# Output projection: a chunk's transposes, weight scaling and operand stores written behind the next chunk's matmuls

## The chip, the core and the metric

The kernel runs on one core of a Trainium2 chip. The metric is the device time of one execution in microseconds (us). The engines named below are PE (matmuls and transposes; PEld is its weight load), DVE (elementwise work and reductions), ACT (scalar engine: casts, squares, scaling by a column), POOL (small vectors here) and SP, whose queue issues the DMAs. Each engine works through its own list of instructions in order.

## The reference, cut to what matters

One encoder block on 2048 tokens of width 1024. Two mixers give `y1` (1024 columns) and `y2` (512 columns). What follows them is the part that this change touches:

```python
h = h + jnp.concatenate([y_ssd, y_s5], axis=-1) @ w_out[i]
h = h + conv_ffn(rms_norm(h, norm_ffn_w[i]), ffn_w_up[i], ffn_conv_w[i],
                 ffn_conv_b[i], ffn_w_down[i])
return rms_norm(h, norm_final_w)
```

`rms_norm` divides a row by the root of its mean square and multiplies it by a weight per column; `conv_ffn` is an up projection, a convolution of width 3, a gate and a down projection.

## The kernel before

The program has three long parts: the mixers (up to about 1200 us), the output projection (16 chunks of 128 tokens, 1206 to 1620 us) and the FFN (the rest). The change lies in the second part and at its border to the third. Below, G0 to G15 are the matmuls of the 16 chunks.

**One chunk of the output projection.** `out_pre` prepares the left operand. It loads `z`, `y`, `c` and the decay of the chunk, multiplies `c` by the running state `fst` on PE (tile `po`, 8 products, two records each), adds that to `y` (lines 852, 853), carries the state on (lines 862, 863), multiplies by `z` (854), and splits the result into a high and a low part (`yh` on ACT, `yl` on DVE, lines 443, 444; the 512 columns of `y2` in lines 876, 877). It also sums the squares (tiles `sqr`, `pn`, `ssq`) and makes two row factors on POOL (`rsq`). `out_gemm` then runs 72 matmuls of 128x512: 12 blocks of the depth, two halves `n` of the columns, three products each (`yh*wh`, `yh*wl`, `yl*wh`; `mm3`, lines 448 to 450). They end in the four tiles `p1`, `p2` of the two halves. DVE adds them to `x` in `xto` (912, 913), SP stores the sum (914). Then comes the norm in front of the FFN: ACT squares the row and sums it (917), POOL makes the factor (`rstd`, lines 435 to 440), ACT scales the row into `h2` (919).

**The tail of a chunk** is the loop over `q` at the end of `out_gemm`: per half, four PE transposes of `h2` into the one buffer `pth` (927), four scalings by the norm's weight into `hT` (ACT for the first half, line 933; DVE for the second, 931) and one store into `hop_d` (934), the right operand of the FFN. Since `pth` has one buffer, the second four transposes wait until ACT has emptied it. Below, Tc is the pair of transpose blocks of chunk c.

**The FFN** is a list of jobs (`strassen`). The first 22 jobs use tokens 0 to 1023, that is the `hop_d` rows of chunks 0 to 7 and the sums of them that `tok_sums` makes in chunks 9 to 12. The first job needs two blocks of `w_up` (tile `wr`, line 1090) with their sums and splits on DVE and ACT (`left_ops`), and 14 loads `tst` of the right operand (1020), each split into `th` (ACT, 1022) and `tl` (DVE, 1023). The loads of all these parts share one pool of 13 buffers (`tag="g4"`).

**Order.** The program text sets a priority; a scheduler then orders every engine's list ahead of time. In the text, chunk `ch + 1` is prepared before chunk `ch` is multiplied:

```python
for ch in range(15):
    cur = pre
    pre = b.out_pre(sp, gp, ps, pp, ch + 1)
    b.out_gemm(sp, gp, ps, pp, ch, *cur)
```

Of the kernel before, what the change touches and what calls it, by code (L numbers as in the profile page):

```python
# [9 lines left out]
F32 = mybir.dt.float32  # L10
# [4 lines left out]
PSUM = bass.MemoryType.PSUM  # L15
DRAM = bass.MemoryType.DRAM

P = 128
L = 2048
D = 1024  # L20
# [395 lines left out]
NG4 = 13  # L416
# [4 lines left out]
class Block:  # L421
# [476 lines left out]
    def out_gemm(self, sp, sq, ps, pp, ch, yh, yl, rs):  # L898
        nc = self.nc
        v = nc.vector  # L900
        t0 = 128 * ch
        xt = sq.tile([P, D], F32, name="xto", tag="g4", bufs=NG4)
        nc.sync.dma_start(xt, self.A["x"][0, t0:t0 + P, :])
        for n in range(2):
            c = slice(512 * n, 512 * n + 512)
            p1 = ps.tile([P, 512], F32, name="p1", tag="mm")
            for k in range(8):
                self.mm3(p1, (yh[:, k], yl[:, k]), [w[:, k, c] for w in self.wo], k == 0, k == 7)
            p2 = ps.tile([P, 512], F32, name="p2", tag="mm")
            for k in range(4):  # L910
                self.mm3(p2, (yh[:, 8 + k], yl[:, 8 + k]), [w[:, 8 + k, c] for w in self.wo], k == 0, k == 3)
            v.scalar_tensor_tensor(xt[:, c], p1, rs[:, 0:1], xt[:, c], ALU.mult, ALU.add)
            v.scalar_tensor_tensor(xt[:, c], p2, rs[:, 1:2], xt[:, c], ALU.mult, ALU.add)
        nc.sync.dma_start(self.x2_d[t0:t0 + P, :], xt)
        h2 = sp.tile([P, D], F32, name="h2", bufs=2)
        s2 = sp.tile([P, 2], F32, name="ssn", bufs=2)
        nc.scalar.activation(h2, xt, AF.Square, accum_out=s2[:, 0:1])
        self.rstd(s2[:, 1:2], s2[:, 0:1], self.rtmp(sp, "rtmq"), 1.0 / D)
        nc.scalar.activation(h2, xt, AF.Copy, scale=s2[:, 1:2])
        hop = self.hop_d[ch // 8]  # L920
        t1 = 128 * (ch % 4)
        for q in range(2):
            pt = pp.tile([P, 4, P], F32, name="pth", bufs=1)
            cur = sq.tile([P, 4, P], F32, name="hT", tag="g2", bufs=NG2)
            for j in range(4):
                k = 4 * q + j
                nc.tensor.transpose(pt[:, j], h2[:, 128 * k:128 * k + 128], self.ident)
            for j in range(4):
                w = self.nfw[:, 4 * q + j:4 * q + j + 1]
                if q:  # L930
                    v.tensor_scalar(cur[:, j], pt[:, j], w, None, ALU.mult)
                else:
                    nc.scalar.activation(cur[:, j], pt[:, j], AF.Copy, scale=w)
            nc.sync.dma_start(hop[:, (5 if q else 7) if ch % 8 > 3 else q, :, t1:t1 + P], cur)
# [92 lines left out]
    def strassen(self, pu, pd, sp, jobs):  # L1027

        nc = self.nc
        copy = lambda src: self.copied(sp, src)  # L1030
        def prod(ps, j, o, first):
            kt, mm = j["kt"], nc.tensor.matmul
            for k in range(kt):
                l, r = j["L"][o](k), j["R"][o](k)
                for i, (x, y) in enumerate(((l[0], r[0]), (l[0], r[1]), (l[1], r[0]))):
                    mm(ps, x, y, start=first and k == i == 0, stop=k == kt - 1 and i == 2, skip_group_check=not first)  # L1036
        def first(j):
            j["A"] = pu.tile([P, 512], F32, name="pA", bufs=2)
            prod(j["A"], j, 0, True)
            p1 = copy(j["A"])  # L1040
            pD = pu.tile([P, 512], F32, name="pD", bufs=2)
            prod(pD, j, 1, True)
            j["take"](0, 0, pD, p1)
        def middle(j):
            prod(j["A"], j, 2, False)
            j["u2"] = copy(j["A"])
            j["B"] = pd.tile([P, 512], F32, name="pB", bufs=2)
            prod(j["B"], j, 3, True)
            prod(j["A"], j, 4, False)
            j["take"](1, 1, j["B"], copy(j["A"]))  # L1050
        def end(j):
            prod(j["A"], j, 5, False)
            j["take"](0, 1, j["A"], None)
            prod(j["B"], j, 6, False)
            j["take"](1, 0, j["B"], j["u2"])
            j["done"]()
        prev = R = None
        jobs[0]["L"] = jobs[0]["left"]()
        for i, j in enumerate(jobs):
            if j["right"]:  # L1060
                if prev:
                    end(prev)
                prev = None
                R = j["right"]()
            j["R"] = R
            if i + 1 < len(jobs):
                jobs[i + 1]["L"] = jobs[i + 1]["left"]()
            first(j)
            if prev:
                end(prev)  # L1070
            middle(j)
            prev = j
            if j.get("after"):
                j["after"]()
        end(prev)
# [108 lines left out]
def hybrid_block_kernel(ctx: ExitStack, tc: tile.TileContext, *aps):  # L1184
    nc = tc.nc
    A = dict(zip(_INS, aps[:-1]))
    b = Block(nc, tc, A, aps[-1])
    pool = tc.tile_pool
    right = lambda name: tc.tile_pool(name=name, bufs=1, side="right")
# [4 lines left out]
    with ExitStack() as mix:  # L1194
        en = mix.enter_context
        mc = en(pool(name="mixc", bufs=1))
# [3 lines left out]
        pp = psa.enter_context(pool(name="pp", bufs=1, space=PSUM, side="right"))  # L1200
        ps, p5 = (psg.enter_context(pool(name=n, bufs=2, space=PSUM)) for n in ("psmm", "ps5"))
# [39 lines left out]
        with pool(name="s5v", bufs=1) as vp, ExitStack() as xs:  # L1241
# [7 lines left out]
            sp = rs.enter_context(right("sp"))  # L1249
# [39 lines left out]
        ps = psb.enter_context(pool(name="psb", bufs=4, space=PSUM))  # L1289
        rs.close()  # L1290
        psa.close()
        pp = psc.enter_context(pool(name="ppb", bufs=1, space=PSUM, side="right"))
        gp = en(tc.tile_pool(name="gp", bufs=1, side="right", reuse_waits="tile"))
        with right("b1") as sp:
            pre = b.out_pre(sp, gp, ps, pp, 0)
            for ch in range(15):
                cur = pre
                pre = b.out_pre(sp, gp, ps, pp, ch + 1)
                b.out_gemm(sp, gp, ps, pp, ch, *cur)
                if 9 <= ch < 13:  # L1300
                    b.tok_sums(gp, 0, ch - 9)
            b.ffn_consts(mc, gp, ps)
            b.out_gemm(sp, gp, ps, pp, 15, *pre)
        wo.close()
        psb.close()
        pu = en(pool(name="psu", bufs=4, space=PSUM))
# [4 lines left out]
        b.ffn_late(fs)  # L1311
        jobs = [b.up_job(ft, gp, fs, s, f) for s in range(2) for f in range(b.NF)]
        jobs += [b.down_job(ft, gp, fs, c, i) for c in range(3) for i in range(8)]
        b.strassen(pu, pd, fs, jobs)


# [34 lines left out]
```

## Time and profile before

| | |
|---|---|
| median of 3 runs | 2987.97 us (2986.86 to 2992.83) |
| the profiled execution | 2995.89 us, span in the trace 2994.1 us |
| PE busy over the span | 2743.8 us (92%), 12952 matmul records |
| DVE, ACT, POOL busy | 2213.7, 1365.9, 659.3 us (74%, 46%, 22%) |
| mean granted clock of PE | 0.959 of full speed |
| output projection, first matmul of G0 to last of G15 | 1205.87 to 1609.76 us |
| first matmul of the FFN | 1619.65 us |

The span is what the trace covers of the profiled execution; the rest of its time lies around it. Matmuls are pipelined, so the distance from one start to the next tells more than the duration of one record. A granted clock of 1 stands for 2.4 GHz, 0.5 for 1.2 GHz; values between are means over a stretch.

### The profile page before, as it was taken

To read this page: it belongs to the slowest core of one execution; us is meant where nothing else is said; L and a number is where in the kernel's file an instruction comes from. 1 tells how busy PE (TensorE), PEld (TensorE's weight loads), DVE (VectorE), ACT (ScalarE), POOL (GpSimd) and SP (SyncE) were. 2 spreads that over 40 slices of the span, in tenths; PEclk is the share of its full clock that TensorE was granted. 3 is DMA by queue.
4 is the path that set the end of the run, shared out by engine and by line. 5 is a ranking of instruction groups with operands and counts; after the bars stand their busy time and mean duration, and the time that the engine had idled before them with its cause. 6 is when DMAs were issued, how large, how long until landed. Compare 5 with 4: busy or idle time off the path is not lost. (4 is left out here: it accounts for less than half of the span.)

```text
span 2994.1 us, 37277 instructions
## 1 busy us (share of the span) xinstructions
PE 2743.8 (92%) x12952; PEld 2196.2 (73%) x12952; DVE 2213.7 (74%) x3287; ACT 1365.9 (46%) x2329; POOL 659.3 (22%) x1133
## 2 busy tenths in 40 slices
PE   6999899787999997787988999999999999999997
PEld 4556899665878886676766887787877877877775
DVE  5997488786787776655766777778878878656586
ACT  4532355455567665333334444446444445233254
POOL 0543299993133322112111000000000000000012
PEclk9999999887999999898889999999999999999999
DMA  4545734448456656956865223425433446565464
GB/s 126 166 120 157 199 101 125 111 138 221 130 164 175 189 162 209 224 162 176 223 192 163 78 94 118 134 85 189 148 113 126 134 134 216 178 204 189 150 222 152
DMA packets 507145, 471.55 MB, mean 157 GB/s; under 512 B 90108, under 2 KB 417100, under 8 KB 506956
## 3 DMA queue, kind: packets, MB, share of 16 engines
q1 hardware_dynamic: 504716, 463.99, 51.8%
q0 software_dynamic: 2240, 5.18, 0.7%
q8 instruction: 102, 1.67, 0.2%
q14 instruction: 87, 0.71, 0.1%
HBM read 324.37 MB, written 144.67 MB: 157 GB/s over the span
## 5 line engine op out<-in xcount | busy, mean ns | idle before, releaser
L1036 PE MATMUL pA<-th,lh 128*128 128x512 f32 x1056 | 424.5, 403 | 36.2 <-ACT pc L1079 34.0
L1036 PE MATMUL pA<-tl,lh 128*128 128x512 f32 x1056 | 421.6, 399 | 2.4 <-DVE tl L1023 2.3
L1036 PE MATMUL pA<-th,ll 128*128 128x512 f32 x1056 | 420.8, 399 | 1.5 <-DVE ll L444 1.4
L448 PE MATMUL pmm<-hh,wh 128*128 128x512 f32 (+1 forms) x896 | 335.2, 374 | 6.3 <-DVE zt L709 3.1
L449 PE MATMUL pmm<-hl,wh 128*128 128x512 f32 (+1 forms) x896 | 334.8, 374 | 0.0
L450 PE MATMUL pmm<-hh,wl 128*128 128x512 f32 (+1 forms) x896 | 331.7, 370 | 0.0
L1036 PEld LDWEIGHTS pA<-th,lh 128*128 128x128 f32 x1056 | 201.4, 191 | 96.3 <-ACT pc L1079 46.1
L1036 PEld LDWEIGHTS pA<-tl,lh 128*128 128x128 f32 x1056 | 201.8, 191 | 51.1 <-DVE tl L1023 4.7
L1036 PEld LDWEIGHTS pA<-th,ll 128*128 128x128 f32 x1056 | 201.2, 191 | 50.5 <-DVE ll L444 2.7
L1036 PE MATMUL pB<-tl,lh 128*128 128x512 f32 x528 | 208.8, 395 | 2.6 <-DVE tl L1023 2.6
L1036 PE MATMUL pB<-th,lh 128*128 128x512 f32 x528 | 208.6, 395 | 1.6 <-ACT lh L443 1.6
L1036 PE MATMUL pB<-th,ll 128*128 128x512 f32 x528 | 208.3, 395 | 0.0
L448 PEld LDWEIGHTS pmm<-hh,wh 128*128 128x128 f32 x896 | 170.6, 190 | 37.3 <-issue 5.7
L1079 ACT COPY pc<-pA 128x512 f32<-128x512 f32 x204 | 114.8, 581 | 181.2 <-PE pA L1036 180.6
L449 PEld LDWEIGHTS pmm<-hl,wh 128*128 128x128 f32 x896 | 170.5, 190 | 26.2 <-issue 5.9
L450 PEld LDWEIGHTS pmm<-hh,wl 128*128 128x128 f32 x896 | 170.4, 190 | 24.5 <-issue 4.4
L767 ACT ACTIVATE Lt<-rw,tokS 128x128 f32<-128x128 f32 x512 | 157.6, 389 | 56.9 <-PE pyd L773 44.9
L695 DVE SCALAR_TENSOR_TENSOR xbc<-rb,cw,xbc 128x1024 f32<-128x1024 f32 x128 | 176.0, 1378 | 3.5 <-ACT xbc L693 2.4
L448 PE MATMUL p<-wo,yh 128*128 128x512 f32 x384 | 162.3, 423 | 13.8 <-ACT yh L443 13.8
L443 ACT CAST lh<-s 128x512 fp32r<-128x512 f32 (+3 forms) x136 | 109.9, 815 | 126.7 <-DVE s L1003 63.2
L444 DVE TENSOR_TENSOR ll<-s,lh 128x1024 fp32r<-128x1024 f32 (+3 forms) x136 | 126.2, 931 | 49.5 <-PE pA L1036 41.3
L449 PE MATMUL p<-wo,yh 128*128 128x512 f32 x384 | 160.4, 418 | 0.0
(421 smaller groups left out, 6206.2 us busy)
## 6 DMA issues: line engine op xcount, KB each, us to landing
wr<-in_ffn_w_up_dram SPq DMA_DIRECT2D x88, 512.0 KB
rw<-acs_d SPq DMA_DIRECT2D x128, 256.0 KB
wraw<-in_w_in_dram SPq DMA_DIRECT2D x52, 512.0 KB
ar<-act_d SPq DMA_DIRECT2D x32, 512.0 KB
yp_d<-cv SPq DMA_DIRECT2D x32, 512.0 KB
cv<-yp_d SPq DMA_DIRECT2D x32, 512.0 KB
tst<-hop_d SPq DMA_DIRECT2D x28, 512.0 KB
act_d<-cv SPq DMA_DIRECT2D x22, 512.5 KB
```

The costliest lines, as they stand in the source:

```text
L443: self.nc.scalar.copy(hi, src)
L444: self.nc.vector.tensor_tensor(lo, src, hi.bitcast(F32), ALU.subtract)
L448: mm(ps, lhs[0], rhs[0], start=first, stop=False)
L449: mm(ps, lhs[0], rhs[1], start=False, stop=False)
L450: mm(ps, lhs[1], rhs[0], start=False, stop=last)
L695: nc.vector.scalar_tensor_tensor(ac, rb[:, j:j + 1024], cw(j), ac, ALU.mult, ALU.add)
L767: nc.scalar.activation(Lt[:, d, h], rw[:, d, h], AF.Exp, bias=tk(0, d, h))
L1036: mm(ps, x, y, start=first and k == i == 0, stop=k == kt - 1 and i == 2, skip_group_check=not first)
L1079: self.nc.scalar.copy(t, src)
```

## The change

The loop over `q` becomes a function of its own, `out_tail`. In the text the tail of chunk `ch - 1` now stands behind the matmuls of chunk `ch`; the tail of chunk 15 is called in the middle of the first FFN job, and its `h2` takes a buffer of the shared pool, since its own pool is closed by then. `pth` gets a PSUM pool of its own that stays open. `ffn_consts` moves ahead of the last chunk's matmuls and `tok_sums` one chunk later.

```diff
         nc.sync.dma_start(self.x2_d[t0:t0 + P, :], xt)
-        h2 = sp.tile([P, D], F32, name="h2", bufs=2)
+        if ch < 15:
+            h2 = sp.tile([P, D], F32, name="h2", bufs=2)
+        else:
+            h2 = sq.tile([P, D], F32, name="h2", tag="g4", bufs=NG4)
...
+        return h2
+
+    def out_tail(self, sq, pt_, ch, h2):
...
         for q in range(2):
-            pt = pp.tile([P, 4, P], F32, name="pth", bufs=1)
+            pt = pt_.tile([P, 4, P], F32, name="pth", bufs=1)
...
             first(j)
+            if j.get("mid"):
+                j["mid"]()
             if prev:
...
+        pth = en(pool(name="pth", bufs=1, space=PSUM, side="right"))
...
-            for ch in range(15):
+            h2 = None
+            for ch in range(16):
                 cur = pre
-                pre = b.out_pre(sp, gp, ps, pp, ch + 1)
-                b.out_gemm(sp, gp, ps, pp, ch, *cur)
-                if 9 <= ch < 13:
-                    b.tok_sums(gp, 0, ch - 9)
-            b.ffn_consts(mc, gp, ps)
-            b.out_gemm(sp, gp, ps, pp, 15, *pre)
+                if ch < 15:
+                    pre = b.out_pre(sp, gp, ps, pp, ch + 1)
+                else:
+                    b.ffn_consts(mc, gp, ps)
+                last, h2 = h2, b.out_gemm(sp, gp, ps, pp, ch, *cur)
+                if ch:
+                    b.out_tail(gp, pth, ch - 1, last)
+                if 10 <= ch < 14:
+                    b.tok_sums(gp, 0, ch - 10)
...
+        jobs[0]["mid"] = lambda: b.out_tail(gp, pth, 15, h2)
```

The scheduler decides what this does to each list. First PE, before, from the last matmuls of chunk 3 to the first of chunk 4 (`p_11778` is a result tile of chunk 3, `p_11892` and `p_11917` of chunk 4, `h_11794` is `h2` of chunk 3):

```order
L448 MATMUL p_11778<-wo_10988,yh 128x512
L449 MATMUL p_11778<-wo_10989,yh 128x512
L450 MATMUL p_11778<-wo_10988,yl 128x512
L849 MATMUL po<-ctt,fst 128x128 x8
L927 MATMUL pth<-ident,h_11794 128x128 x8
L448 MATMUL p_11892<-wo_10988,yh 128x512
L449 MATMUL p_11892<-wo_10989,yh 128x512
L448 MATMUL p_11917<-wo_10988,yh 128x512
```

All eight transposes of chunk 3 stand between the two chunks, right behind the state products `po`. The odd chunks 1 to 13 read like this; the tails of the even chunks 0 to 14 stand as two blocks of four among the next chunk's matmuls already.

Now PE after the change: first around the state products inside chunk 4 (`p_11913`, one of its result tiles), then from chunk 4 (`p_11938`) to chunk 5 (`p_12052`, `p_12077`), with `h_11775` the `h2` of chunk 3.

```order
L448 MATMUL p_11913<-wo_10988,yh 128x512
L449 MATMUL p_11913<-wo_10989,yh 128x512
L849 MATMUL po<-ctt,fst 128x128 x8
L450 MATMUL p_11913<-wo_10988,yl 128x512
L448 MATMUL p_11913<-wo_10988,yh 128x512
L449 MATMUL p_11913<-wo_10989,yh 128x512
```

The products stand 25 matmuls ahead of the chunk's end, and the left operand of chunk 5 hangs on them. From the end of chunk 4 on:

```order
L449 MATMUL p_11938<-wo_10989,yh 128x512
L450 MATMUL p_11938<-wo_10988,yl 128x512
L936 MATMUL pth<-ident,h_11775 128x128 x4
L448 MATMUL p_12052<-wo_10988,yh 128x512
L449 MATMUL p_12052<-wo_10989,yh 128x512
L448 MATMUL p_12077<-wo_10988,yh 128x512
```

A first block of transposes still stands between two chunks, but it is that of the chunk before; the second block follows 20 matmuls later. The tails of chunks 1, 5, 9 and 11 keep a row of eight, one chunk later than before. Behind the state products of a chunk stand, up to the next chunk's first matmul, 25 matmuls in chunks 4, 5, 8 and 9, 21 and a row of eight in chunk 12, 13 and a row of eight in chunk 6, 6 and a row of eight in chunk 2; in chunk 10 it is 5 matmuls, a row of eight and the state products of one more chunk. In chunks 0, 1, 3, 7, 11 and 13 they stand earlier; chunk 14's have 23 behind them, and no chunk follows the next. Behind G15 stand five transposes of chunk 14 and four of chunk 15, then the FFN's first 110 matmuls, then the last four transposes.

Then SP's queue from the end of the output projection into the FFN, before:

```order
L914 DMA x_d<-xto 128x1024
L1090 DMA wr<-in_ffn_w_up_dram 128x8x128 x2
L934 DMA hop_d<-hT 128x4x128
L840 DMA ctt<-ct_d 128x4x128
L934 DMA hop_d<-hT 128x4x128
L1020 DMA tst<-hop_d 128x1024 x2
L914 DMA x_d<-xto 128x1024
L1020 DMA tst<-hop_d 128x1024
L934 DMA hop_d<-hT 128x4x128
L1020 DMA tst<-hop_d 128x1024
L934 DMA hop_d<-hT 128x4x128
L985 DMA nlw<-in_norm_final_w_dram 128x1024
```

and after the change:

```order
L943 DMA hop_d<-hT 128x4x128 x2
L994 DMA nlw<-in_norm_final_w_dram 128x1024
L914 DMA x_d<-xto 128x1024
L943 DMA hop_d<-hT 128x4x128
L1101 DMA wr<-in_ffn_w_up_dram 128x8x128 x2
L943 DMA hop_d<-hT 128x4x128
L1029 DMA tst<-hop_d 128x1024 x14
L1101 DMA wr<-in_ffn_w_up_dram 128x8x128 x4
L943 DMA hop_d<-hT 128x4x128 x2
```

`nlw` is the load that can only start when G15 has ended. Before, the first two loads `wr` and four loads `tst` stand ahead of it; now all of them stand behind it, and behind the store of chunk 15's `xto`.

Last DVE at the same border, before (`p_13943` is the last result tile of chunk 15):

```order
L913 SCALAR_TENSOR_TENSOR xto<-p_13943,rsq,xto 128x512
L931 TENSOR_SCALAR hT<-pth,nfw 128x128 x4
L1003 TENSOR_TENSOR s_14016<-wr,s_14015 128x512
L1023 TENSOR_TENSOR tl_14038<-tst,th_14037 128x1024 x2
L1023 TENSOR_TENSOR tl_14048<-tst,th_14047 128x1024 x2
```

and after the change (`p_13924` is the last result tile of chunk 15):

```order
L913 SCALAR_TENSOR_TENSOR xto<-p_13924,rsq,xto 128x512
L940 TENSOR_SCALAR hT<-pth,nfw 128x128 x4
L1009 TENSOR_TENSOR s_13996<-wr 128x512
L1010 TENSOR_TENSOR s_13996<-s_13996,wr 128x512
L1011 TENSOR_TENSOR wr<-wr 128x512
L444 TENSOR_TENSOR ll<-wr,lh 128x1024
L1012 TENSOR_TENSOR s_13997<-wr,s_13996 128x512
L444 TENSOR_TENSOR ll<-s_13996,lh 128x1024
L444 TENSOR_TENSOR ll<-wr,lh 128x1024
L444 TENSOR_TENSOR ll<-s_13997,lh 128x512
L1032 TENSOR_TENSOR tl_14019<-tst,th_14018 128x1024 x2
```

The sums and splits of the first job's left operand, which stood among the work of chunks 14 and 15, now stand behind the last addition of chunk 15 and ahead of the first `tl`.

## Rows read from the trace of the kernel before

**Rows 1.** Engines' busy time by stretches; then PE's granted clock, DMA share, GB/s.

```profile
1205.87:1609.76 403.89, 352.53 (x1612) 286.64 (x1612) 252.11 (x408) 127.50 (x239) 77.74 (x202) 0.89 0.67 184
1445.91:1497.47 51.56, 44.23 (x197) 36.11 (x195) 34.88 (x57) 16.43 (x30) 8.58 (x23) 0.83 0.91 239
```

**Rows 2.** Whom PE waited for, 1205 to 1620 us: total, times, longest.

```profile
PE pth L927 <- ACT h L919: 38.6, 7, 6.5
PE p L448 <- ACT yh L443: 13.8, 3, 9.8
PE pth L927 <- ACT hT L933: 9.9, 8, 1.2
PE po L849 <- DMA ctt<-ct_d: 5.3, 2, 3.4
```

**Rows 3.** PE in order of time, inside chunk 1: start, us, line [idle before].

```profile
1237.71 0.60 PE L927 MATMUL pth<-ident,h 128*128 128x128 f32 x4
1238.07 0.48 PE L448 MATMUL p<-wo,yh 128*128 128x512 f32 x1
```

**Rows 4.** The same from the end of chunk 1 into chunk 2.

```profile
1246.30 1.95 PE L849 MATMUL po<-ctt,fst 128*128 128x128 f32 x16
1254.69 1.12 PE L927 MATMUL pth<-ident,h 128*128 128x128 f32 x4 [6.45 <-ACT h L919]
1257.04 1.12 PE L927 MATMUL pth<-ident,h 128*128 128x128 f32 x4 [1.23 <-ACT hT L933]
1257.97 0.79 PE L448 MATMUL p<-wo,yh 128*128 128x512 f32 x1
...
1262.76 0.40 PE L448 MATMUL p<-wo,yh 128*128 128x512 f32 x1
1262.99 0.39 PE L449 MATMUL p<-wo,yh 128*128 128x512 f32 x1
```

**Rows 5.** PE, DVE and ACT in order of time, chunk 3 to chunk 4.

```profile
1297.78 1.95 PE L849 MATMUL po<-ctt,fst 128*128 128x128 f32 x16
1297.98 0.75 DVE L913 SCALAR_TENSOR_TENSOR xto<-p,rsq,xto 128x512 f32<-128x512 f32 x1 [0.50 <-PE p L450]
1302.54 1.22 DVE L863 TENSOR_TENSOR fst<-fst,sft 128x1024 f32<-128x1024 f32 x1
1303.67 1.22 DVE L854 TENSOR_TENSOR yt<-yt,ztt 128x1024 f32<-128x1024 f32 x1
1304.97 1.15 ACT L919 ACTIVATE h<-xto,ssn 128x1024 f32<-128x1024 f32 x1 [5.06 <-POOL ssn L440]
1308.34 1.06 ACT L443 CAST yh<-yt 128x1024 fp32r<-128x1024 f32 x1
```

**Rows 6.** PE in order of time in the FFN: two single waits, and what follows.

```profile
1887.56 0.50 PE L1036 MATMUL pA<-th,lh 128*128 128x512 f32 x1 [1.61 <-ACT pc L1079]
1887.90 0.39 PE L1036 MATMUL pA<-tl,lh 128*128 128x512 f32 x1
...
2413.08 0.80 PE L1036 MATMUL pA<-th,lh 128*128 128x512 f32 x1 [2.83 <-ACT pc L1079]
2413.68 0.63 PE L1036 MATMUL pA<-tl,lh 128*128 128x512 f32 x1
```

**Rows 7.** SP, DVE and PE in order of time: the first job's loads and start.

```profile
1564.89 1.00 SPq L1090 DMA_DIRECT2D wr<-in_ffn_w_up_dram  x2
1570.83 0.69 DVE L1000 TENSOR_TENSOR s<-wr 128x512 f32<-128x512 f32 x1 [0.16 <-DMA wr<-in_ffn_w_up_dram]
...
1609.36 0.40 PE L450 MATMUL p<-wo,yl 128*128 128x512 f32 x1
1620.11 5.76 DVE L1023 TENSOR_TENSOR tl<-tst,th 128x1024 fp32r<-128x1024 f32 x5
1621.38 0.79 PE L1036 MATMUL pA<-tl,lh 128*128 128x512 f32 x1 [0.96 <-DVE tl L1023]
1633.16 4.68 DVE L1023 TENSOR_TENSOR tl<-tst,th 128x1024 fp32r<-128x1024 f32 x4
```

More of the change, by code (lines that the diff above doesn't have):

```diff
@@ L919, in out_gemm @@
         nc.scalar.activation(h2, xt, AF.Copy, scale=s2[:, 1:2])
+        return h2
+    def out_tail(self, sq, pt_, ch, h2):
+        nc = self.nc
+        v = nc.vector
         hop = self.hop_d[ch // 8]
```

## The prediction

> **What bounds the kernel now.** I read four views: the windows by stage, the waits of PE, PE's own rows in order of time around a chunk's border, and the loads at the border to the FFN. PE is busy for 92% of the span, but not evenly. In the output projection it works 352.53 of 403.89 us [rows 1], so 51.4 us are idle, at a mean granted clock of 0.89, while the DMA engines have a share of 0.67. The reader should see that PE is the bound here and loses time to waits. Of the waits up to 1620 us [rows 2], 38.6 us go to `h2` (7 times, five of them near 6.5 us), 9.9 us to the one buffer `pth` (8 times 1.23 us), 4.0 us to `yh` (13.8 less the 9.76 before G0 starts), and 5.3 us to the loads `ctt`. Both transpose waits belong to the odd chunks, whose eight transposes stand between two chunks; nothing else is ahead of PE there.
>
> Such a handover costs more than its wait. In the middle of a chunk, four transposes delay the next matmul by 0.36 us [rows 3]. At the end of chunk 1 they start 6.45 us late, then 1.23 us late, and the two blocks take 1.12 + 0.93 us beside these waits, some 1.3 us more than 2 x 0.36 [rows 4]. Then 11 matmuls need 4.79 us (1257.97 to 1262.76) where the pace of 0.233 us that follows would give 2.57 [rows 4]: 0.43 us apiece, the lower of the clock's two levels, 1.2 instead of 2.4 GHz. So a handover pays about 1.3 + 2.2 = 3.5 us of slow clock on top of its idle time; with seven (odd chunks 1 to 13) 25 us.
>
> **What the change removes.** The tail of a chunk now comes a chunk later, so its `h2` is old when the transposes are reached, and the waits on `h2` in the stage go. That leaves nothing of the 51.4 us idle unless something new waits, and nothing of the 25 us: 76 us at most by these rows. I leave 2.5 of the 5.3 us for `ctt` in place, since no edit touches these loads: 73.5.
>
> **What it puts in their place.** The long wait also covered something: while PE stood still, DVE finished the next chunk's left operand. Take chunk 3 [rows 5]: `po` starts at 1297.78, the last product `yt` ends at 1303.67 + 1.22 = 1304.89, 7.1 us later; the cast to `yh` takes 1.06 us, 8.2 us in all (in the rows it runs later, at 1308.34, since ACT is busy with `h2` and `hT` first). In the new list of DVE one more addition `xto` (0.75) stands ahead of that product: 8.9 us from `po` to the next chunk's first matmul. What PE has to do in that time is read from the order: `po` itself 1.95 us, the matmuls behind it at 0.233, four transposes 0.4, or a row of eight 2.0 (2 x 0.36 and 1.23 for `pth`).
>
> - Chunks 4, 5, 8, 9 (25 matmuls): cover 1.95 + 5.8 + 0.4 = 8.1, wait 0.8 each, 3.2.
> - Chunk 6 (13 and a row): 1.95 + 3.0 + 2.0 = 6.9, wait 2.0.
> - Chunk 2 (6 and a row): 1.95 + 1.4 + 2.0 = 5.3, wait 3.6.
> - Chunk 10: more stands in DVE's chain, and the second `po` needs the new state, whose update ends 1302.54 + 1.22 - 1297.78 = 6.0 us behind `po` even in [rows 5]. With one more `xto` and a sum (0.7 each) and four scalings (1.2) in the chain I get 2.4 us for the state and 2.2 for `yh`: 4.6.
> - Chunk 12: 1.95 + 4.9 + 2.0 = 8.8, wait 0.1. The rest have cover enough.
>
> Together 13.5 us. The four rows of eight that stay (chunks 1, 5, 9, 11) keep their 1.23 us: 4.9.
>
> Does the clock fall behind these? The FFN has two single waits to compare [rows 6]. Behind 1.61 us the next matmul lasts 0.39 us, full pace; behind 2.83 us it lasts 0.63, the slow one. So I charge nothing behind 0.8 us, and a handover's 3.5 us at the ends of chunks 2, 6 and 10, where the waits add up to 3 us and more with that for `pth`: 10.5. Bounds: none of the three (+10.5 us gained), or all seven as before (14 lost).
>
> The gain in the stage is 73.5 - 13.5 - 4.9 - 10.5 = 44.6 us. The moved scalings and stores themselves cost nothing extra: as many as before, on ACT and DVE, which work 127.50 and 252.11 of 403.89 us [rows 1]; without that cover the scalings of a chunk would show, about 2.3 us.
>
> **The FFN's start.** The second FFN matmul, the first that needs `tl`, begins at 1621.38 [rows 7], 11.6 us behind G15's end (1609.36 + 0.40). Before, `wr` is issued at 1564.89 and used at 1570.83 [rows 7]; `left_ops` and four `tst` lie under G14 and G15, which hide them. In the new order `wr` stands behind `nlw` and the stores of chunks 14 and 15, all held by G15's end. I estimate the issue 2.2 us behind that end: a last addition of 0.75 and four scalings of chunk 14, near 1.2 as the casts of [rows 5], stand ahead of it, and then the queue's own steps. Then 5.9 us until it can be used, as in [rows 7]; then `left_ops`, now ahead of the first `tl` on DVE: four sums of 0.69, three splits near 1.22, one of 0.68, 7.1 us; then `tl`, 1.2. That is 16.4 against 11.6, a loss of 5. All `tst` stand behind `wr` too; `th` on ACT waits for them, and PE for `th`. The bounds: 0, if the loads come at once and DVE starts sooner, and some 25, if the 14 `tst` drip in.
>
> A page speaks against this part: the Trainium skill, "DMA: Bandwidth & Descriptors", section "Rules for kernel authors", says to issue a DMA early, compute, and wait late, so that its fixed cost is hidden. The 5.9 us from issue to use, hidden before [rows 7], agree. [...]
>
> **Sum.** 44.6 gained, 5 lost: 39.6. The profiled execution took 2995.89 us (span 2994.1); 2956.3 remain. It was 7.9 us longer than the median of 2987.97, so the median should fall to about 2948.
>
> **The rivals.**
> *The operand chain takes the place of `h2`.* If PE has less cover than the order suggests, or DVE and ACT are late when `po` is done (ACT's `yh` stands behind casts and squares of other chunks), each of seven handovers waits some 4.5 us and keeps its 3.5 us of slow clock: 7 x 8 = 56 of the 76 us remain, and 5 at the FFN: 15 gained, 2973. For it: 8.9 us of chain against 8.1 of cover is close. Against it: DVE is idle for 152 us of the stage [rows 1]. Chance 0.15.
>
> *Nearly everything is won.* If the short waits leave the clock alone and the FFN's start is hidden, 60 to 70 us: 2918 to 2928. For it [rows 6], first pair; against it 1.95 + 1.4 us of cover at chunk 2. Chance 0.1.
>
> *Nothing.* The stage could be bound by its transfers: 403.89 us at 184 GB/s are 74 MB, and if that rate is the most it can have, the loads only wait elsewhere: 2988, or 2993 with the FFN's start. Against it: 239 GB/s with a share of 0.91 in a busy stretch, by which 74 MB take 311 us [rows 1]. Chance 0.06.
>
> *Slower.* The loads `tst` share 13 buffers with the rest of the border, among them chunk 15's `h2`. Before, the 14 ended at 1633.16 + 4.68 = 1637.84, 17.7 us from the first `tl` at 1620.11 [rows 7]. If only one buffer were free, each would take a load (5.9), a cast (1.06) and a split (1.2): 8.2 us, 115 for 14, a loss of 97 beside the 5; that leaves 57 lost: 3045. With two buffers it is 57 us for 14, a loss of 45 in all, the point where it eats the gain; with three, some 25. For it: a `tst` now cannot start before G15 ends, so none is ahead. Against it: what else used the pool is nearly done by then. Chance 0.07. The rule of the Trainium skill on early issue ("DMA: Bandwidth & Descriptors", as above) is on the side of this rival.
>
> **How the numbers follow.** My forecast has 0.62; its own range, from the bounds of the clock (+10.5, -14) and of the FFN's start, is 2930 to 2966. With the better case and the larger part of the first rival, 2918 to 2976 holds 8 in 10. Faster by over 0.2% (6 us, about what can be told from no change) sums to 0.62 + 0.15 + 0.1, and a rest of 0.01 from the third: 0.88; same 0.05; slower 0.07.
>
> **What the profile after would show.** If right: the waits of the transposes on `h2` are gone but one or two at the border; the stage from G0's first matmul to G15's last takes 355 to 365 us at a clock above 0.94 and over 200 GB/s; new waits `p` on `yh` or `po` on `fst` of 2 to 5 us at the ends of chunks 2, 6, 10, under 1 us at 4, 5, 8, 9; four waits of 1.23 us for `pth`; the second FFN matmul 15 to 18 us behind G15's end, with DVE at `left_ops`. Wrong: a row of waits on `yh` as long as those on `h2` (the first rival); waits on DMA in the stage (the third); PE waiting for `th` again and again in the first job, on loads 8 us apart (the fourth).

## The result and the profile after

Four executions of the changed kernel beside four of the kernel before: the medians are 2953.02 and 2990.4 us, 37 us apart; the ratio of the executions is 0.9859 (95% interval 0.9837 to 0.9881), by which the gain is 42 us. Two more sets of executions below give 40 and 35 us by their medians. 2948 was predicted, a gain of 40 us, with 2918 to 2976 as the range. The profile that was taken with this result fell into an execution in which PE's granted clock was 0.568 throughout (4353.75 us), so the rows below are of another execution of the same kernel (`after_again`, 2954.72 us, span 2952.9 us).

The windows: G0's first matmul to G15's end, then from there to the second FFN matmul. Columns as in [rows 1].

```profile
1205.09:1561.22 356.13, 334.33 (x1608) 273.35 (x1608) 246.06 (x398) 120.54 (x232) 66.30 (x202) 0.96 0.72 199
1561.22:1579.44 18.22, 2.65 (x12) 1.43 (x10) 9.66 (x15) 10.20 (x15) 1.66 (x9) 0.59 0.87 282
```

The stage is 403.89 - 356.13 = 47.8 us shorter. PE is idle in it for 21.8 us instead of 51.4, and it is busy for 18.2 us less, at a clock of 0.96 instead of 0.89, with the same matmuls but five transposes (some 0.5 us of work, now behind G15): that second part is slow clock that is gone. The border grew from 11.6 to 18.2 us. Together 415.51 [rows 1, 7] became 374.35, 41.2 us less, as much as the two profiled executions differ (2995.89 against 2954.72).

Whom PE waits for between 1205 and 1580 us, the view of [rows 2]:

```profile
PE p L448 <- ACT yh L443: 19.7, 8, 9.5
PE pA L1045 <- ACT th L1031: 9.2, 1, 9.2
PE pth L936 <- ACT hT L942: 6.2, 5, 1.2
PE pth L936 <- ACT h L922: 3.6, 1, 3.6
PE po L849 <- DVE fst L863: 3.3, 1, 3.3
PE pn L887 <- DVE sqr L883: 1.8, 1, 1.8
...
```

The 38.6 us on `h2` of [rows 2] have become one wait of 3.6, and that one lies behind G15. What is left in the stage is `yh` (19.7 less 9.5 ahead of G0), the buffer `pth`, the state `fst`, and at the start of chunk 12 the sums of squares `sqr` and an addition `xto`. In order of time, at the ends of chunks 2, 4 and 10 and the start of chunk 12, with the wait in brackets:

```profile
1263.03 2.02 PE L849 MATMUL po<-ctt,fst 128*128 128x128 f32 x16 [0.23 <-DMA ctt<-ct_d]
1268.13 0.66 PE L936 MATMUL pth<-ident,h 128*128 128x128 f32 x4 [1.24 <-ACT hT L942]
1272.01 0.79 PE L448 MATMUL p<-wo,yh 128*128 128x512 f32 x1 [3.23 <-ACT yh L443]
...
1316.37 0.50 PE L448 MATMUL p<-wo,yh 128*128 128x512 f32 x1 [1.65 <-ACT yh L443]
1316.71 0.39 PE L449 MATMUL p<-wo,yh 128*128 128x512 f32 x1
...
1450.06 3.76 PE L849 MATMUL po<-ctt,fst 128*128 128x128 f32 x16 [3.26 <-DVE fst L863]
...
1474.60 0.38 PE L887 MATMUL pn<-ones,sqr 128*128 128x1 f32 x2 [1.85 <-DVE sqr L883]
1476.93 0.76 PE L448 MATMUL p<-wo,yh 128*128 128x512 f32 x1 [0.97 <-DVE xto L912]
1477.49 0.63 PE L449 MATMUL p<-wo,yh 128*128 128x512 f32 x1
```

Behind 1.65 us the next matmul lasts 0.39 us, full pace. Behind 3.23 us the first lasts 0.79 instead of 0.50, and behind 3.26 the state products last 3.76 instead of the 1.95 of [rows 4]: there the clock had fallen. It had fallen too at the start of chunk 12, where PE stood still twice, for 1.85 and 0.97 us, with six matmuls of one column between: the matmuls behind last 0.63 us.

### The profile page after: what moved, and what is told of

It reads as the page before. It is cut to its first block, busy times and chain, and to the rows that moved or that the text cites. A ratio compares the mean times of both kernels' runs of the same rounds, so it can differ in the third digit from the quotient of the medians.

```text
span 4352.0 us, 37281 instructions
## 1 busy us (share of the span) xinstructions
PE 4237.3 (97%) x12952; PEld 2628.4 (60%) x12952; DVE 2197.4 (50%) x3287; ACT 1366.3 (31%) x2329; POOL 568.5 (13%) x1133
## 4 chain that ended last, share of the span: by engine, by line
PE 95%; DMA 2%; DVE 1%; ACT 1%; issue 0%; SPq 0%; POOL 0%; ACTq 0%; POOLq 0%; DVEq 0%
PE pA L1045 27%; PE pB L1045 13%; PE pmm L448 7%; PE pmm L449 7%; PE pmm L450 7%; PE pD L1045 7%; PE p L448 3%; PE p L449 3%; PE p L450 3%; PE s5py L390 2%; PE pst L794 2%; PE s5pk L279 1%; PE pyd L773 1%; PE pu L450 1%; PE pu L448 1%; PE pu L449 1%
## 5 line engine op out<-in xcount | busy, mean ns | idle before, releaser
L1045 PE MATMUL pA<-th,lh 128*128 128x512 f32 x1056 | 587.0, 557 | 15.3 <-ACT th L1031 9.2
L1045 PE MATMUL pA<-tl,lh 128*128 128x512 f32 x1056 | 587.9, 557 | 1.6 <-DVE tl L1032 1.6
L1045 PE MATMUL pA<-th,ll 128*128 128x512 f32 x1056 | 585.3, 555 | 0.0
L449 PE MATMUL pmm<-hl,wh 128*128 128x512 f32 (+1 forms) x896 | 478.7, 534 | 0.0
L448 PE MATMUL pmm<-hh,wh 128*128 128x512 f32 (+1 forms) x896 | 477.9, 533 | 0.0
L450 PE MATMUL pmm<-hh,wl 128*128 128x512 f32 (+1 forms) x896 | 474.0, 529 | 0.0
L1045 PE MATMUL pB<-tl,lh 128*128 128x512 f32 x528 | 294.3, 557 | 1.6 <-DVE tl L1032 1.6
L1045 PE MATMUL pB<-th,ll 128*128 128x512 f32 x528 | 293.6, 556 | 0.0
L448 PE MATMUL p<-wo,yh 128*128 128x512 f32 x384 | 223.8, 583 | 12.6 <-ACT yh L443 12.5
L449 PE MATMUL p<-wo,yh 128*128 128x512 f32 x384 | 223.8, 583 | 0.0
L450 PE MATMUL p<-wo,yl 128*128 128x512 f32 x384 | 219.7, 581 | 0.0
```

Source lines behind the costliest of these rows:

```text
L448: mm(ps, lhs[0], rhs[0], start=first, stop=False)
L449: mm(ps, lhs[0], rhs[1], start=False, stop=False)
L450: mm(ps, lhs[1], rhs[0], start=False, stop=last)
```

## The experiments

Stage is G0's first matmul to G15's end, border from there to the second FFN matmul, both in us in each run's profile. Ratios are to the kernel before on the same chip.

| run | stage | border | ratio (95% interval) |
|---|---|---|---|
| before | 403.9 | 11.6 | |
| after_again | 356.1 | 18.2 | 0.9862 (0.9835 to 0.9889) |
| after_third | 355.2 | 18.4 | 0.9893 (0.9874 to 0.9913) |
| stage_alone | 357.3 | 12.3 | 0.9866 (0.9831 to 0.9900) |
| border_alone | 402.1 | 17.7 | 1.0058 (1.0041 to 1.0075) |
| h2_sooner_in_before | 384.0 | 10.5 | 0.9966 (0.9950 to 0.9982) |
| h2_sooner_after | 354.7 | 17.8 | 0.9876 (0.9855 to 0.9897) |
| operand_chain_short | 354.8 | 18.2 | 0.9873 (0.9853 to 0.9893) |
| operand_chain_short_in_before | 411.1 | 11.6 | 1.0031 (1.0017 to 1.0044) |
| early_wr | 358.4 | 10.3 | 0.9865 (0.9847 to 0.9883) |
| both_edits | 358.8 | 9.8 | 0.9865 (0.9847 to 0.9884) |
| early_wr_no_nlw | 355.9 | 9.1 | 0.9877 (0.9857 to 0.9897) |
| early_wr_nlw_in_stage | 355.8 | 8.8 | 0.9862 (0.9839 to 0.9884) |

**The changed kernel again.** The same kernel twice more, with the times beside those of the kernel before.

> The changed kernel once more, for a profile at the usual clock and a closer ratio. By the prediction: 2948 us beside 2988 (ratio 0.9866); the stage from G0's first matmul to G15's last 355 to 365 us at a granted clock above 0.94; no wait of the transposes on h2 inside it; waits on yh or on the state of 2 to 5 us at the ends of chunks 2, 6 and 10 and near 0.8 us at 4, 5, 8 and 9; four waits of 1.23 us for pth; the second FFN matmul 15 to 18 us behind G15's end. By the first rival (the operand chain in place of h2) seven waits near 4.5 us on yh. By the slower rival the first FFN job waits for tst again and again; its time is already excluded.

Stage, border and waits are as shown above. The third time:

> The changed kernel a third time, beside the run before in this list, on the same chip: ratio to before 0.986 (0.984 to 0.988); the stage 356 us and the second FFN matmul 18 us behind G15's end.

It gave 355.2 and 18.4 us. Its profiled execution took 2966.95 us, 12 more than the other: G0 began at 1213.97 instead of 1205.09, and behind the border it took 1377.62 instead of 1373.46 us. Neither lies in what the change touches. So an execution's whole time scatters by some 10 us, while stage and border of these two profiles repeat within 1 us. Edits of 6 us are judged by the windows below, not by the ratio; each window is that of one profiled execution.

**The two halves of the change apart.** `stage_alone` keeps the delayed tails and puts chunk 15's tail back behind G15, with its `h2` in the pool of the others:

```diff
-        if ch < 15:
-            h2 = sp.tile([P, D], F32, name="h2", bufs=2)
-        else:
-            h2 = sq.tile([P, D], F32, name="h2", tag="g4", bufs=NG4)
+        h2 = sp.tile([P, D], F32, name="h2", bufs=2)
...
                     b.tok_sums(gp, 0, ch - 10)
+            b.out_tail(gp, pth, 15, h2)
...
-        jobs[0]["mid"] = lambda: b.out_tail(gp, pth, 15, h2)
```

> The tails stand one chunk later as in the change, but chunk 15's whole tail is called right behind G15, inside the output projection, and its h2 lies in the pool of the others. In the order the engines' lists of chunks 0 to 13 are those of the change, and wr and four tst stand ahead of nlw again. Theory (the border costs 5 us): 5 us faster than the changed kernel (ratio to before 0.985 if that has 0.9866), the second FFN matmul 11 to 12 us behind G15's end. Rival A (the border is hidden or neutral): within 1.5 us of the changed kernel. Rival B (the border is where the change wins, since the wait of chunk 15's transposes on h2 goes): 5 us or more slower than the changed kernel.

`border_alone` delays only chunk 15's tail:

```diff
-                if ch:
-                    b.out_tail(gp, pth, ch - 1, last)
+                if ch < 15:
+                    b.out_tail(gp, pth, ch, h2)
```

> Only the last chunk's tail goes into the first FFN job; the tails of chunks 0 to 14 are called right behind their own matmuls as before the change. In the order the lists of the stage are nearly those of the kernel before; wr and all tst stand behind nlw. Theory: 5 us slower than before (ratio 1.0017), the second FFN matmul 16 us behind G15's end; 25 us slower if the tst drip in. Rival A: ratio 1.000. Rival B: 5 us or more faster, 0.998.

In the windows the halves come apart cleanly. The first has the whole gain of the stage and the short border of before:

```profile
1201.84:1559.13 357.29, 334.34 (x1606) 273.64 (x1607) 250.82 (x404) 123.57 (x235) 70.58 (x202) 0.96 0.75 207
1559.13:1571.42 12.29, 4.08 (x17) 2.33 (x15) 4.79 (x12) 7.33 (x15) 1.66 (x9) 0.74 0.70 212
```

The second has the stage of before and the long border:

```profile
1200.34:1602.47 402.13, 347.59 (x1612) 282.17 (x1612) 247.70 (x402) 124.22 (x236) 73.40 (x202) 0.91 0.64 177
1602.47:1620.18 17.71, 1.89 (x6) 1.00 (x5) 8.53 (x11) 9.30 (x11) 1.66 (x9) 0.58 0.84 272
```

So the tails of chunks 0 to 14 make the gain, and chunk 15's costs 6 us at the border; the earlier `ffn_consts`, the later `tok_sums` and the pool of `pth`, which `border_alone` has too, do next to nothing for the stage (402.1 against 403.9). In the whole time the 6 us do not show for `stage_alone`, whose executions lie between 2947.84 and 2965.15. `border_alone` came out 0.6% slower, which is more than its windows explain (419.8 against 415.5 us): its profiled execution of 2994.8 us was the shortest of nine, and where the others spent 10 to 22 us more stays open. So the halves add up in the windows (46.6 us gained and 6.1 lost, against 41.2 for the whole change) but not in the whole times (ratios 0.9866 and 1.0058, against 0.9862).

**How much the wait on h2 is worth alone.** In both kernels four of the six POOL instructions between the sum of squares and `h2` go:

```diff
-        self.rstd(s2[:, 1:2], s2[:, 0:1], self.rtmp(sp, "rtmq"), 1.0 / D)
+        q = self.rtmp(sp, "rtmq")
+        nc.gpsimd.tensor_scalar(q[:, 0, 0:1], s2[:, 0:1], 1.0 / D, EPS, ALU.mult, ALU.add)
+        nc.gpsimd.tensor_tensor(s2[:, 1:2], q[:, 0, 0:1], self.neghalf[:, 0:1], ALU.pow)
```

> The kernel before the change with a shorter way to h2: four of the six small POOL instructions behind the sum of squares are left out (the step that refines the inverse root; its result changes a little), so h2 comes some 3.9 us sooner. In the order the eight transposes of the odd chunks still stand between po and the next chunk. Theory (the wait on h2 covers the operand chain of 8.2 to 8.9 us behind po): of 6.45 us per handover some 2.5 remain on h2, new waits of up to 1.5 us on yh come behind them, and 2 to 3 us are gained at each of five handovers and one or two of slow clock: the stage 385 to 395 us instead of 404, ratio to before 0.994 to 0.997. Rival (h2 alone holds PE): the whole 3.9 us at each, and the clock with it, stage below 380, ratio 0.991 or less.

At the handover from chunk 3 to 4 the rows of PE and ACT in order of time read:

```profile
1291.93 1.95 PE L849 MATMUL po<-ctt,fst 128*128 128x128 f32 x16
1296.36 0.66 PE L929 MATMUL pth<-ident,h 128*128 128x128 f32 x4 [2.48 <-ACT h L921]
1298.24 1.11 PE L929 MATMUL pth<-ident,h 128*128 128x128 f32 x4 [1.23 <-ACT hT L935]
1299.07 1.04 ACT L443 CAST yh<-yt 128x1024 fp32r<-128x1024 f32 x1 [0.88 <-DVE yt L854]
1300.17 0.80 PE L448 MATMUL p<-wo,yh 128*128 128x512 f32 x1 [0.81 <-ACT yh L443]
```

The wait on `h2` is 3.97 us shorter than the 6.45 of [rows 4], and 0.81 of it comes back as a wait on `yh`, which was not there before. Five handovers have these three waits. The cast to `yh` now waits for nothing but DVE's last product, and the next chunk begins 1300.17 - 1291.93 = 8.24 us behind `po`, the 8.2 us of the predicted chain: a still earlier `h2` could hardly shorten such a handover. The stage falls by 19.9 us, 1 us more than the theory's range, ratio 0.9966. So the wait on `h2` did cover the operand chain, and with `po` right ahead of the transposes an early `h2` is worth some 20 us. The change wins 47.8 us; in its order `po` also stands further ahead of the chunk's end. How much of the other 28 us each of the two, the old `h2` and the place of `po`, would bring alone is not shown.

> The same four POOL instructions left out in the changed kernel (the lists of the stage shift somewhat). Theory (the tail comes a chunk later, h2 is old by then): no gain in the stage, 352 to 360 us; the wait of chunk 15's transposes on h2 behind G15 falls, but the first FFN matmul waits for wr all the same: within 4 us of the changed kernel. Rival (h2 still ends waits somewhere in the changed kernel): 8 us or more gained.

In the changed kernel the same edit gives 1.5 us in the stage and 0.4 at the border, not the rival's 8. The run is a weak test, though: in its shifted lists tails stand earlier at the ends of chunks 2 and 11, and PE waits for `h2` twice in the stage, 4.0 and 6.0 us. That `h2` is old when it is used is shown by the changed kernel's own waits, of which none in the stage is on `h2`.

**A shorter operand chain.** The product with `z` moves ahead of `po`:

```diff
+                if not q:
+                    v.tensor_tensor(ef, ef, zt, ALU.mult)
+                    v.tensor_tensor(yt, yt, zt, ALU.mult)
                 v.tensor_tensor(e4, e4, po, ALU.mult)
                 v.tensor_tensor(yt[:, 4 * q:4 * q + 4], yt[:, 4 * q:4 * q + 4], e4, ALU.add)
-        v.tensor_tensor(yt, yt, zt, ALU.mult)
+        else:
+            v.tensor_tensor(yt, yt, zt, ALU.mult)
```

> The changed kernel with a shorter chain from the state products to yh: y and the decay are multiplied by z before the products are there, so that behind po only two multiplications, two additions and the cast are left (1.2 us of DVE less in the chain, one instruction of 1.2 us more per chunk outside it). In the order PE's po now has 17 to 42 matmuls behind it and only the tails of chunks 4 and 14 stand as rows of eight. Theory (PE's waits in the stage are the operand chain, 13.5 us, the rows of eight, 4.9, and slow clock behind the longer ones, up to 10): no wait on yh over 0.3 us, at most two of 1.23 us for pth, the stage 335 to 343 us instead of 356, the kernel 13 to 20 us faster than the changed one (ratio to before 0.980). Rival (something else ends these waits: ACT's place, ctt, the pn sums): the waits go to another name and the kernel gains under 5 us.

The theory missed and the rival came out: the stage won 1.4 us, and PE's waits in it went on to other names and places:

```profile
PE p L448 <- ACT yh L443: 20.4, 8, 10.0
PE p L448 <- DVE xto L916: 5.7, 1, 5.7
PE pth L940 <- ACT hT L946: 2.8, 2, 1.6
PE p L448 <- ACT yh L880: 0.6, 1, 0.6
```

That is 19.5 us without the 10.0 ahead of G0, after 21.5. Two things changed beside the chain. The scheduler made new lists: at the end of chunk 7, for one, only 16 matmuls and four transposes stand behind `po`. And the moved multiplication of the decay (`ef`) by `z` is often not done when `po` is there, because DVE waits for the load of the decay, as this line of DVE's waits and the rows of chunk 7 show:

```profile
DVE ef L853 <- DMA ef<-eac_d: 17.1, 10, 3.2
```

```profile
1380.27 1.95 PE L849 MATMUL po<-ctt,fst 128*128 128x128 f32 x16
1383.91 1.23 DVE L853 TENSOR_TENSOR ef<-ef,ztt 128x1024 f32<-128x1024 f32 x1 [3.22 <-DMA ef<-eac_d]
1390.59 0.79 PE L448 MATMUL p<-wo,yh 128*128 128x512 f32 x1 [4.20 <-ACT yh L443]
```

There the chain from `po` to the next chunk took 10.3 us instead of getting shorter. In the changed kernel DVE waits at this place for `po`, 16.4 us in all, and not for that load. The run therefore does not isolate the chain's price.

> The same shorter chain in the kernel before the change, where the eight transposes of the odd chunks still stand between the chunks and still wait for h2 (in the order PE's rows around them are those of before). Theory (the long wait on h2 covers the operand chain there): the waits on h2 stay near 6.5 us, those on yh (4 us in all) go, the stage 398 to 405 us, ratio to before 0.998 to 1.001. Rival (the handover is bound by the operand chain already, and h2 only stands first in the list): 10 us or more gained, as in the changed kernel.

Here too both missed, the rival by its sign: the stage grew by 7.2 us. The waits on `h2`, which were to stay near 6.5 us each, fell to 9.3 in all, since PE, held by `ctt`, comes to the transposes later. PE's waits, then those of SP's queue, in that stage:

```profile
PE po L849 <- DMA ctt<-ct_d: 20.7, 6, 6.2
...
PE pth L931 <- ACT h L923: 9.3, 4, 4.7
```

```profile
SPq L864 <- DVE ef L853: 32.3, 7, 7.3
```

The load `sft` (864) takes a buffer that the new multiplication `ef` (line 853 of this kernel) has to free, and waits for it in SP's queue seven times. In five of the six cases in which `ctt` is late, it is the next load behind such a stop: in one, the multiplication ends at 1299.45, `sft` is issued at 1299.47, `ctt` at 1300.37, and PE waits 2.13 us for it. So this run does not say what the wait on `h2` covers; that rests on `h2_sooner_in_before`.

**The border.** `early_wr` calls the first job's left operand ahead of G15:

```diff
                     b.ffn_consts(mc, gp, ps)
+                    L0 = b.up_job(None, gp, None, 0, 0)["left"]()
...
+        jobs[0]["left"] = lambda: L0
```

> The changed kernel with the loads and sums of the first FFN job's left operand called ahead of G15 in the text; chunk 15's tail stays inside the first job. In the order wr is issued two chunks earlier and left_ops are done under G15; nlw and all tst still stand behind G15's end. Theory (the border loses its time to wr, which waits for G15's end, and to left_ops on DVE behind it): the second FFN matmul comes 10 to 12 us behind G15's end instead of 18, the kernel 6 to 8 us faster than the changed one. Rival (the loads tst and nlw share the queue and are the limit): 15 us or more behind G15's end, under 3 us gained.

The border fell from 18.2 to 10.3 us as the theory had it; the stage took 358.4, so the stretch from G0 to the second FFN matmul is 5.6 us shorter. The ratio, 0.9865, does not tell it from the changed kernel's, so the 6 to 8 us of the whole time are not shown.

> Both edits in the changed kernel: the short operand chain and the early wr. Theory: the two gains add, as they lie in different stretches: 20 to 27 us faster than the changed kernel, ratio to before 0.977 to 0.979, near 2925 us beside 2992. Rival (both release the same resource, the transfers near the border or the pool of buffers): no more than the larger of the two alone.

The stage 358.8 and the border 9.8 us; together 5.8 us less than the changed kernel, as with `early_wr` alone, since the short chain wins nothing.

> The changed kernel with the first job's left operand called ahead of G15, and nlw loaded before chunk 0 in place of behind G15. In the order PE's list of chunks 4 to 15 is that of the run with wr alone; no load of the FFN but the tst stands behind G15's end. Theory (with wr early, the second FFN matmul waited for the tst behind nlw's 0.5 MB and the store of x2): 8 to 10 us behind G15's end instead of 18 in the changed kernel and 10.3 with wr alone; the kernel 6 to 9 us faster than the changed one if the stage keeps its length. Rival (the FFN's later jobs give it back): the second matmul sooner, the kernel within 2 us of the changed one.

The border is 9.1 us, and the stage 355.9. But `nlw` ahead of chunk 0 is paid elsewhere: G0 waits 15.8 us for its first operand instead of 9.5, and the median, 2957.74 us, is within 2 us of that of `after_third` on the same chip (2959.04), as the rival said. The last run puts it a few chunks later (beside the edit of `early_wr`):

```diff
-        self.nlw = cst.tile([P, D], F32, name="nlw")
-        self.nc.sync.dma_start(self.nlw, self.A["norm_final_w"].partition_broadcast(P))
...
+                if ch == 4:
+                    b.nlw = gp.tile([P, D], F32, name="nlw")
+                    b.nc.sync.dma_start(b.nlw, b.A["norm_final_w"].partition_broadcast(P))
```

> The changed kernel with the first job's left operand called ahead of G15 and nlw loaded among the loads of the first chunks of the output projection, behind G0's start (in the run that loaded it before chunk 0, G0 waited 15.8 us for its operand instead of 9.5). Theory (these two loads were all that the border had lost): G0 waits 9 to 10 us again, the second FFN matmul 9 to 10 us behind G15's end, the stage 355 to 359 us; 6 to 9 us faster than the changed kernel, ratio to before 0.983 to 0.985. Rival (later parts give it back, or it drowns in the spread of a run): 0.986 to 0.989.

Stage and border take 364.5 us, 9.8 less than in the changed kernel, and the ratio is still 0.9862. G0 waits 13.15 us. SP's queue shows why, in order of time at the start of chunk 0 (`ys_d` is a store of the mixers):

```profile
1201.93 2.63 SPq L411 DMA_DIRECT2D ys_d<-s5vl  x2
1206.67 0.37 SPq L835 DMA_DIRECT2D ztt<-z_d  x1
1207.15 0.52 SPq L837 DMA_DIRECT2D yt<-y_d  x1
1207.76 7.44 SPq L870 DMA_DIRECT2D ysT<-ys_d  x4
```

and the same place in the changed kernel:

```profile
1195.69 0.60 SPq L411 DMA_DIRECT2D ys_d<-s5vl  x1
1196.39 0.44 SPq L835 DMA_DIRECT2D ztt<-z_d  x1
1196.92 0.53 SPq L837 DMA_DIRECT2D yt<-y_d  x1
1197.74 0.60 SPq L411 DMA_DIRECT2D ys_d<-s5vl  x1
```

The loads of chunk 0 stood between the last two stores and now stand behind both. An edit four chunks later moved them in the scheduled queue, and with them some 4 of the 10 us. No version here beats the changed kernel by more than its interval.

## Why the prediction was right, point by point

**The waits removed.** All waits on `h2` in the stage were to go, and went. PE's idle time was to fall from 51.4 to 20.9 us (13.5 for the operand chain, 4.9 for `pth`, 2.5 for `ctt`); it fell to 21.8. One reading of the kernel before was too simple: not all seven handovers were held by `h2`. At the ends of chunks 9 and 11 PE waited for `ctt` and then for `yh`, and 1.0 us in all for `h2`; the chain came out there before the change already:

```profile
1455.28 3.75 PE L849 MATMUL po<-ctt,fst 128*128 128x128 f32 x16 [3.43 <-DMA ctt<-ct_d]
1464.89 0.80 PE L448 MATMUL p<-wo,yh 128*128 128x512 f32 x1 [2.67 <-ACT yh L443]
```

The sum is not touched by it, as it goes by the idle time of the whole stage.

**The operand chain in their place.** 13.5 us were predicted for `yh` and the state, and 10.2 + 3.3 = 13.5 measured. That the sums agree to a tenth is luck: chunks 4, 5, 8 and 9 cost 1.65, 0.56, 1.65 and 1.28 us where 0.8 each was predicted, 1.9 too little in all, and chunks 2, 6 and 10 cost 3.23, 1.60 and 3.26 where 3.6, 2.0 and 4.6 were, 2.1 too much. At chunk 4 a step was missed. PE, DVE and ACT of the changed kernel around its end:

```profile
1314.12 0.60 PE L936 MATMUL pth<-ident,h 128*128 128x128 f32 x4
```

```profile
1313.06 1.22 DVE L854 TENSOR_TENSOR yt<-yt,ztt 128x1024 f32<-128x1024 f32 x1
```

```profile
1314.76 0.63 ACT L942 ACTIVATE hT<-pth,nfw 128x128 f32<-128x128 f32 x2 [13.27 <-PE pth L936]
1315.27 1.04 ACT L443 CAST yh<-yt 128x1024 fp32r<-128x1024 f32 x1
```

`yt` was done at 1313.06 + 1.22 = 1314.28, but the cast to `yh` began at 1315.27: it stands on ACT behind two scalings `hT`, and these wait for transposes that stand on PE behind the last matmul. That is 1 us of the 1.65. The prediction named this danger as the first rival's mechanism, and at chunk 4 it is there, at under a quarter of the 4.5 us that rival needed.

**pth and ctt.** Four waits of 1.23 us for `pth` in the stage, as predicted. `ctt` was left in at 2.5 us and cost 0.2; instead 1.85 us went to the sums of squares `sqr` and 0.97 to `xto` at the start of chunk 12, which the prediction did not have.

**The clock.** Predicted was a net gain of 25 - 10.5 = 14.5 us of slow clock; PE's busy time fell by 18.2. The three long waits were to keep it, at 3.5 us each. The ends of chunks 2 and 10 did and the start of chunk 12 did, which was not foreseen; by the rows each cost some 2.6 us (13 matmuls at 0.43 us apiece in place of 0.233 at chunks 2 and 12). Behind chunk 6 (1.24 and then 1.60 us) the matmuls ran at full pace in this profile. In that of `after_third` the same two waits, 1.23 and 1.60 us, were followed by matmuls of 0.63 us: two executions of one kernel differ there.

**The border.** 16.4 us predicted, 18.2 measured. The mis-sized term is the 5.9 us from issue to use of `wr`. The rows of SP and DVE:

```profile
1562.96 2.79 SPq L1101 DMA_DIRECT2D wr<-in_ffn_w_up_dram  x2
```

```profile
1571.62 0.69 DVE L1009 TENSOR_TENSOR s<-wr 128x512 f32<-128x512 f32 x1 [7.23 <-DMA wr<-in_ffn_w_up_dram]
...
1578.17 7.13 DVE L1032 TENSOR_TENSOR tl<-tst,th 128x1024 fp32r<-128x1024 f32 x6
```

The issue came 1.7 us behind G15's end (2.2 predicted), then 8.7 us to the first use on DVE instead of 5.9, then `left_ops` 6.6 (7.1 predicted) and `tl` 1.3. From the issue of `wr` to that use, first before and then after the change, the windows read:

```profile
1564.89:1570.83 5.94, 4.68 (x14) 3.58 (x15) 2.26 (x5) 4.40 (x11) 0.00 (x0) 0.50 0.87 235
1562.96:1571.62 8.66, 1.38 (x7) 0.74 (x5) 1.13 (x5) 2.78 (x4) 1.51 (x6) 0.60 1.06 314
```

The DMA engines moved 1.4 MB in the first stretch and 2.7 MB in the second, and were busy in both. Ahead of `wr` in the queue now stand `nlw` and two stores, all released by G15's end, 1.25 MB together: by this estimate the 5.9 us of [rows 7] were those of a place with less ahead in the queue. No run takes these three away and leaves the rest, so this cause of the 2.8 us is argued. That the border lacks the early load with its sums is shown by `early_wr`: 10.3 us.

**The rivals.** The stage ran at 199 GB/s instead of 184, so it was not bound by its transfers. The slower rival, `tst` one buffer at a time, did not come: six `tl` run in one piece from 1578.17. The Trainium skill's rule on early issue ("DMA: Bandwidth & Descriptors", section "Rules for kernel authors") had the sign of the border right. The late load lost 6.6 us there, and with the load and its sums early 7.9 us came back (`early_wr`).

**The sum and the range.** The stage won 47.8 us where 44.6 were predicted, and the border lost 6.6 where 5 were; that the total comes within 2 us (41.2 against 39.6) is in part that these two offset each other. Of the signs of being right, four did not come as stated: 199 GB/s in the stage instead of over 200, 18.2 us at the border instead of 15 to 18, over 1 us at chunks 4, 8 and 9, and under 2 at chunk 6. The forecast's own range, 2930 to 2966, does not come out of its bounds: 2948 - 10.5 - 5 is 2932, and 2948 + 14 + 20 is 2982.

## What to carry to other kernels

A long wait can hide a second chain that runs during it. Before pricing its removal, follow the chain from the last common start to the next use, and count from the order how much work stands over it: that gave the size of what came out here, 13.5 us, and `h2_sooner_in_before` shows the same chain as the next limit, 8.24 us behind `po`. Where a scheduler orders the queues, look at the whole order after an edit; a load moved between two chunks can pull loads of a far earlier stage with it, and an edit that shortens one chain can bring a late load into it, or make the scheduler choose another order, and so give the time back.

## What was not expected of the hardware

Slow clock was over a third of what the stage gained: PE was busy 18.2 us less once the waits of 6.45 us were gone. Behind single waits of 1.65 us the next matmul still lasted 0.39 us in both profiles of the changed kernel; two waits close together, 1.2 and 1.6 us at the end of chunk 6, left the matmuls behind them at full pace in one of the two, and in the other they lasted 0.63 us from the third on. The same two profiles, of one kernel, began G0 at 1205.09 and 1213.97 us.
